# RMSNorm with ReLU: loads and stores on one hardware DMA queue in fixed order, 16-row chunks in place in f32, gamma spread on chip

## The chip, the cores and the metric

The kernel runs on one core of a Trainium2 chip. The metric is the device time of one execution in microseconds (us), lower is better. The span of the profile is shorter than the time by about 1.9 us (164.0 and 165.9 us for the kernel before), so large differences can be read from either.

## The reference

```python
x: (16, 1024, 512) f32;  gamma: (512,) f32, ones;  eps = 1e-5
rms = np.sqrt(np.mean(x ** 2, axis=-1, keepdims=True) + eps)
return np.maximum(x / rms * gamma, 0).astype(np.float32)
```

There are 16384 rows of 2 KB. 33.55 MB must be read and 33.55 MB written, 67.1 MB in all, for very little arithmetic.

## The kernel before

Each of the 128 partitions owns 128 neighbouring rows (256 KB). A chunk is 8 rows of every partition, 2 MB; there are 16 chunks. Loads are issued by SyncE (a hardware queue), stores by GpSimd (a software queue that also casts the bf16 result to f32). Gamma is broadcast to all partitions by one DMA at the head of the load queue.

```python
K = 8
gamma_bcast = bass.AP(tensor=gamma.tensor, offset=gamma.offset, ap=[[0, P], gamma.ap[0]])
nc.sync.dma_start(out=gamma_sbuf, in_=gamma_bcast)          # 128 reads of one 2 KB row
# ... cut: eps, scratch, gammaK (gamma repeated K times by a stride of 0)
for i in range(nchunks):                                    # pools of 4 buffers
    s = i * K
    nc.sync.dma_start(out=x_tile, in_=xv[:, s:s + K, :])
    nc.vector.tensor_mul(out=xg, in0=x_tile, in1=gammaK)
    for j in range(K):
        nc.scalar.activation(out=sq_scratch, in_=x_tile[:, j, :], func=Square, accum_out=ss[:, j:j+1])
    nc.scalar.activation(out=rms, in_=ss, func=Sqrt, bias=eps_sbuf, scale=inv_d)
    nc.vector.reciprocal(out=rstd, in_=rms)
    for j in range(K):
        nc.vector.tensor_scalar(out=o_tile[:, j, :], in0=xg[:, j, :], scalar1=rstd[:, j:j+1],
                                scalar2=0.0, op0=mult, op1=max)          # o_tile is bf16
    nc.gpsimd.dma_start(out=ov[:, s:s + K, :], in_=o_tile)               # casts to f32
```

## Time and profile before

| | before |
|---|---|
| time, median of 3 runs | 165.87 us (165.78 to 166.01) |
| span of the profile | 164.0 us |
| bytes moved, mean rate | 67.40 MB, 411 GB/s |
| DVE busy, ACT busy | 122.8 us, 99.4 us |

These lines are from the page of the kernel before. DVE is VectorE, ACT is ScalarE, POOL is GpSimd. The row of digits is the busy share of the 16 DMA engines in 40 equal slices of 4.1 us (9 is 90% or more), and the row under it is what they moved in each.

```profile
span 164.0 us, 565 instructions
DVE 122.8 (75%) x161; ACT 99.4 (61%) x274; POOL 8.9 (5%) x20
...
DMA  5999999999999999999999999999999999998994
GB/s 87 401 420 444 440 412 432 434 432 412 436 436 412 440 434 424 424 432 436 412 436 436 414 432 436 412 440 432 428 424 432 432 416 436 440 432 348 416 420 192
DMA packets 4755, 67.40 MB, mean 411 GB/s; under 512 B 528, under 2 KB 528, under 8 KB 656
...
q1 hardware_dynamic: 2448, 33.82, 57.4%
q0 software_dynamic: 2304, 33.56, 49.4%
...
HBM read 33.82 MB, written 33.55 MB: 411 GB/s over the span
```

The DMA engines are busy in every slice; no compute engine is near full. The first slice is slow (87 GB/s), and the slice at 148 to 152 us has a dip (348). Between them the rate is flat.

From the page's groups of instructions: out<-in, count, busy time, mean ns of one, idle before.

```profile
L70 DVE TENSOR_TENSOR xg<-x_tile,gamma_sbuf 128x4096 f32<-128x4096 f32 x16 | 70.5, 4406 | 29.3 <-DMA x_tile<-in_x_dram 29.3
L84 DVE TENSOR_SCALAR o_tile<-xg,rstd 128x512 bf16<-128x512 f32 x128 | 52.1, 480 | 0.1
```

### The profile page before, as it was taken

What the parts mean: (1) busy time and instruction counts of PE and PEld (TensorE: products, weight loads), DVE (VectorE), ACT (ScalarE), POOL (GpSimd) and SP (SyncE); (2) the same over time, 40 slices, a digit from 0 to 9 for tenths busy, and PEclk for the clock granted to TensorE, in tenths of its full rate; (3) what the DMA queues carried; (4) which work ended last, traced back from release to release, by engine and by line L of the source; (5) the groups of instructions that cost most, each with busy time, mean ns of one, the idle gap of its engine ahead of it and who ended that gap; (6) DMA issues with size and microseconds to landing.
All of it is one profiled execution on the core that took longest, in us unless ns stands there. A gap on an engine that the chain in (4) does not pass through costs nothing.

```text
span 164.0 us, 565 instructions
## 1 busy us (share of the span) xinstructions
DVE 122.8 (75%) x161; ACT 99.4 (61%) x274; POOL 8.9 (5%) x20
## 2 busy tenths in 40 slices
DVE  0029979999999999969498694968949498099600
ACT  3039999999993937739195682928649194094000
POOL 0000010011010101010100001010010101001100
DMA  5999999999999999999999999999999999998994
GB/s 87 401 420 444 440 412 432 434 432 412 436 436 412 440 434 424 424 432 436 412 436 436 414 432 436 412 440 432 428 424 432 432 416 436 440 432 348 416 420 192
DMA packets 4755, 67.40 MB, mean 411 GB/s; under 512 B 528, under 2 KB 528, under 8 KB 656
## 3 DMA queue, kind: packets, MB, share of 16 engines
q1 hardware_dynamic: 2448, 33.82, 57.4%
q0 software_dynamic: 2304, 33.56, 49.4%
q14 instruction: 3, 0.02, 0.0%
HBM read 33.82 MB, written 33.55 MB: 411 GB/s over the span
## 4 chain that ended last, share of the span: by engine, by line
issue 49%; DVE 27%; ACT 8%; DMA 6%; POOL 3%; POOLq 0%; SPq 0%
DVE xg L70 15%; DVE o_tile L84 11%; ACT sq_scratch L74 7%; DMA x_tile<-in_x_dram 6%; POOL out_dram L90 3%; ACT L77 1%; DVE rstd L80 1%; ACT rms L77 0%; POOLq L121 0%; SPq L48 0%; POOLq L90 0%
## 5 line engine op out<-in xcount | busy, mean ns | idle before, releaser
L74 ACT ACTIVATE sq_scratch<-x_tile 128x512 f32<-128x512 f32 x128 | 80.6, 630 | 48.8 <-DMA x_tile<-in_x_dram 45.3
L70 DVE TENSOR_TENSOR xg<-x_tile,gamma_sbuf 128x4096 f32<-128x4096 f32 x16 | 70.5, 4406 | 29.3 <-DMA x_tile<-in_x_dram 29.3
L84 DVE TENSOR_SCALAR o_tile<-xg,rstd 128x512 bf16<-128x512 f32 x128 | 52.1, 480 | 0.1
L74 ACT ACTIVATION_READ_ACCUMULATOR sq_scratch<-x_tile 128x1 f32 x128 | 23.9, 187 | 0.0
L90 POOL DMA_DIRECT2D out_dram<-o_tile x16 | 8.7, 541 | 145.9 <-DVE rstd L80 119.4
L77 ACT ACTIVATE rms<-ss,eps_sbuf 128x8 f32<-128x8 f32 x16 | 4.8, 301 | 0.5
L80 DVE RECIPROCAL rstd<-rms 128x8 f32<-128x8 f32 x16 | 3.1, 196 | 1.2 <-ACT rms L77 1.2
L74 ACT ACT_TABLE_LOAD x1 | 1.3, 1283 | 0.7 <-PEq L107 0.7
L77 ACT ACT_TABLE_LOAD x1 | 1.3, 1283 | 0.0
L51 DVE MEMSET eps_sbuf<- 128x1 f32 x1 | 0.1, 59 | 0.8 <-PEq L107 0.8
L107 POOL MEMSET const-float32-0.0<- 128x1 f32 x1 | 0.1, 99 | 0.2 <-issue 0.2
L107 POOL MEMSET const-bfloat16-1.0<- 128x1 bf16 x1 | 0.1, 102 | 0.0
L107 POOL MEMSET const-float32-1.0<- 128x1 f32 x1 | 0.1, 99 | 0.0
L107 POOL MEMSET const-uint8-127<- 128x1 uint8 x1 | 0.1, 99 | 0.0
## 6 DMA issues: line engine op xcount, KB each, us to landing
x_tile<-in_x_dram SPq DMA_DIRECT2D x16, 2048.0 KB, 26.4
out_dram<-o_tile POOLq DMA_DIRECT2D x16, 2048.0 KB, 21.3
gamma_sbuf<-in_gamma_dram SPq DMA_DIRECT2D x1, 256.0 KB, 5.4
```

Source lines behind the costliest of these rows:

```text
L51: nc.vector.memset(eps_sbuf, eps)
L70: nc.vector.tensor_mul(out=xg, in0=x_tile, in1=gammaK)
L74: nc.scalar.activation(out=sq_scratch, in_=x_tile[:, j, :], func=mybir.ActivationFunctionType.Square, accum_out=ssj)
L77: nc.scalar.activation(out=rms, in_=ss, func=mybir.ActivationFunctionType.Sqrt, bias=eps_sbuf, scale=inv_d)
L80: nc.vector.reciprocal(out=rstd, in_=rms)
L84: nc.vector.tensor_scalar(out=o_tile[:, j, :], in0=xg[:, j, :], scalar1=rj, scalar2=0.0, op0=mybir.AluOpType.mult, op1=mybir.AluOpType.max,)
L90: nc.gpsimd.dma_start(out=ov[:, s:s + K, :], in_=o_tile)
L107: nc = _bacc.Bacc("TRN2", target_bir_lowering=False, num_devices=1)
```

## The change

The intent is to keep the DMA engines in one direction at a time and never without work. All loads and stores go through SyncE's queue, in an order fixed by hand: six loads of 4 MB fill six slots, then store 0, store 1, load 6, store 2, load 7, stores 3 to 7. Chunks have 16 rows, and the work is done in place in f32, so no cast is needed. Gamma comes as four rows, one to partition 0, 32, 64 and 96, and a shuffle on DVE spreads each over its 32 partitions.

```diff
-    K = 8
+    K = 16
+    G = 8
+    nslots = 6
-    nc.sync.dma_start(out=gamma_sbuf, in_=gamma_bcast)
+    for q in range(0, P, 32):
+        nc.scalar.dma_start(out=gseed[q:q + 1, :], in_=gamma[None, :])
+    nc.vector.stream_shuffle(gamma_sb, gseed, [0] * 32)
# ... cut: tiles; the squares' scratch output is now in PSUM ("junk")
+    def load(i):
+        nc.sync.dma_start(out=slot[i % nslots], in_=xv[:, i * K:(i + 1) * K, :])
+    def store(i):
+        nc.sync.dma_start(out=ov[:, i * K:(i + 1) * K, :], in_=slot[i % nslots])
-        nc.gpsimd.dma_start(out=ov[:, s:s + K, :], in_=o_tile)
+    def compute(i):                     # in place in xt = slot[i % nslots], 8 rows at a time:
+        # 8 squares, Sqrt (ACT); xt *= gamma, reciprocal, 8 scalings with max 0 (DVE)
+    for i in range(min(nslots, nchunks)):
+        load(i)
+    for i in range(min(nslots, nchunks)):
+        compute(i)
+    nxt = nslots
+    for i in range(nchunks):
+        store(i)
+        if i >= 1 and nxt < nchunks:
+            load(nxt)
+            compute(nxt)
+            nxt += 1
```

More of the change, by code (lines that the diff above doesn't have):

```diff
@@ L6 @@
 from concourse._compat import with_exitstack
+F32 = mybir.dt.float32
+ALU = mybir.AluOpType
+ACTF = mybir.ActivationFunctionType
 @with_exitstack
@@ L23 @@
     n, d = x2.shape
-    assert n % P == 0
-    rows_per_part = n // P
+    rows = n // P
     inv_d = 1.0 / d
@@ L29 @@
     ov = out2.rearrange("(p r) d -> p r d", p=P)
-    K = 8
-    nchunks = rows_per_part // K
-    assert rows_per_part % K == 0
-    BF = mybir.dt.bfloat16
-    F32 = mybir.dt.float32
-    singles = ctx.enter_context(tc.tile_pool(name="singles", bufs=1))
-    pool = ctx.enter_context(tc.tile_pool(name="pool", bufs=4))
-    small = ctx.enter_context(tc.tile_pool(name="small", bufs=4))
-    gamma_sbuf = singles.tile([P, d], F32)
-    gamma_bcast = bass.AP(
-        tensor=gamma.tensor,
-        offset=gamma.offset,
-        ap=[[0, P], gamma.ap[0]],
-    )
@@ L48 @@
-    nc.sync.dma_start(out=gamma_sbuf, in_=gamma_bcast)
-    eps_sbuf = singles.tile([P, 1], F32)
-    nc.vector.memset(eps_sbuf, eps)
-    sq_scratch = singles.tile([P, d], F32)
-    gammaK = bass.AP(tensor=gamma_sbuf.tensor, offset=gamma_sbuf[:].offset,
-                     ap=[gamma_sbuf[:].ap[0], [0, K], gamma_sbuf[:].ap[1]])
-    for i in range(nchunks):
-        s = i * K
-        x_tile = pool.tile([P, K, d], F32)
-        nc.sync.dma_start(out=x_tile, in_=xv[:, s:s + K, :])
-        rstd = small.tile([P, K], F32)
-        rms = small.tile([P, K], F32)
-        ss = small.tile([P, K], F32)
-        xg = pool.tile([P, K, d], F32)
-        o_tile = pool.tile([P, K, d], BF)
-        nc.vector.tensor_mul(out=xg, in0=x_tile, in1=gammaK)
-        for j in range(K):
-            ssj = ss[:, j:j + 1]
-            nc.scalar.activation(out=sq_scratch, in_=x_tile[:, j, :],
-                                 func=mybir.ActivationFunctionType.Square,
-                                 accum_out=ssj)
-        nc.scalar.activation(out=rms, in_=ss,
-                             func=mybir.ActivationFunctionType.Sqrt,
-                             bias=eps_sbuf, scale=inv_d)
-        nc.vector.reciprocal(out=rstd, in_=rms)
-        for j in range(K):
-            rj = rstd[:, j:j + 1]
-            nc.vector.tensor_scalar(
-                out=o_tile[:, j, :], in0=xg[:, j, :],
-                scalar1=rj, scalar2=0.0,
-                op0=mybir.AluOpType.mult, op1=mybir.AluOpType.max,
-            )
-        nc.gpsimd.dma_start(out=ov[:, s:s + K, :], in_=o_tile)
@@ new lines @@
+    K = 16
+    G = 8
+    nchunks = rows // K
+    nslots = 6
+    ngroups = K // G
+    singles = ctx.enter_context(tc.tile_pool(name="singles", bufs=1))
+    slots = ctx.enter_context(tc.tile_pool(name="slots", bufs=1))
+    small = ctx.enter_context(tc.tile_pool(name="small", bufs=1))
+    psum = ctx.enter_context(
+        tc.tile_pool(name="psum", bufs=1, space=bass.MemoryType.PSUM))
+    ctx.enter_context(tc.manual_schedule())
+    gseed = singles.tile([P, d], F32, name="gseed")
+    gamma_sb = singles.tile([P, d], F32, name="gamma_sb")
@@ new lines @@
+    eps_sb = singles.tile([P, 1], F32, name="eps_sb")
+    junk = psum.tile([P, d], F32, name="junk")
+    slot = [slots.tile([P, K, d], F32, name=f"slot{s}") for s in range(nslots)]
+    ss = [small.tile([P, K], F32, name=f"ss{i}") for i in range(nchunks)]
+    rms = [small.tile([P, K], F32, name=f"rms{i}") for i in range(nchunks)]
+    rstd = [small.tile([P, K], F32, name=f"rstd{i}") for i in range(nchunks)]
+    def load(i):
+        nc.sync.dma_start(out=slot[i % nslots], in_=xv[:, i * K:(i + 1) * K, :])
@@ new lines, in store, with gammaG @@
+    def store(i):
+        nc.sync.dma_start(out=ov[:, i * K:(i + 1) * K, :], in_=slot[i % nslots])
+    def gammaG():
+        g = gamma_sb[:]
+        return bass.AP(tensor=g.tensor, offset=g.offset,
+                       ap=[g.ap[0], [0, G], g.ap[1]])
+    def compute(i):
+        xt = slot[i % nslots]
+        for g in range(ngroups):
+            a, b = g * G, (g + 1) * G
+            for j in range(a, b):
+                nc.scalar.activation(out=junk, in_=xt[:, j, :], func=ACTF.Square,
+                                     accum_out=ss[i][:, j:j + 1])
+            nc.scalar.activation(out=rms[i][:, a:b], in_=ss[i][:, a:b],
+                                 func=ACTF.Sqrt, bias=eps_sb, scale=inv_d)
+            nc.vector.tensor_mul(out=xt[:, a:b, :], in0=xt[:, a:b, :], in1=gammaG())
+            nc.vector.reciprocal(out=rstd[i][:, a:b], in_=rms[i][:, a:b])
+            for j in range(a, b):
+                nc.vector.tensor_scalar(
+                    out=xt[:, j, :], in0=xt[:, j, :],
+                    scalar1=rstd[i][:, j:j + 1], scalar2=0.0,
+                    op0=ALU.mult, op1=ALU.max)
@@ new lines @@
+    nc.vector.memset(gseed, 0.0)
+    nc.vector.memset(eps_sb, eps)
+    for q in range(0, P, 32):
[6 more added lines that the diff above has]
+    nxt = nslots
+    for i in range(nchunks):
+        store(i)
[3 more added lines that the diff above has]
+            nxt += 1
```

## The prediction

> What bounds the kernel: data movement. The page's slice row shows DMA at 9 or more nearly throughout and 411 GB/s over a span of 164.0 us; DVE is busy 122.8 us (75%), ACT 99.4 us (61%). 67.1 MB must move in any case. By the view of stretches, loads alone (11 to 24 us) ran at 432 GB/s, loads and stores mixed from two queues (70 to 110 us) at 427. At 432 the bytes take 155.4 us, so only 8.6 us are to be had:
> - start, about 3.7 us: the first packet starts at 1.75 us, full rate comes at 5.5, because gamma's 128 copies of a 2 KB row go first on the load queue. By the packet records 2.4 us worth of bytes is lost there;
> - mixing, about 1.3 us (1% of some 115 us);
> - a hole at 151 us, about 1.5 us: the last load's data ended at 139.1 us but its waiter on DVE started only at 143.1, DVE then needed 11.3 us, and the store queue ran dry;
> - end, 1.8 us from the last byte (162.15 us).
>
> What the change does. Gamma comes as four rows on ACT's queue and a shuffle on DVE: x loads start the load queue, 2 us won. One queue in fixed order doesn't mix directions: 1 us won. The last transfers are stores whose data is ready, so the hole goes: 1.5 us won. Stores read f32 instead of casting bf16; the HBM bytes are the same and I cost them the same. The Trainium skill ("DMA: Bandwidth & Descriptors", "Issuing engines are not separate DMA queues") says all queues run on the same 16 engines, so one queue can hold the full rate; the trace agrees (432 by one, 427 by two).
>
> Is compute early enough? In place, the multiplication by gamma must now wait for the eight squares of its half chunk. Per 8 rows DVE costs 4.43 + 0.12 + 3.25 us, period 7.57 us (chain of waits, 25 to 62 us); ACT 6.3 us. I expect scaling to f32 to cost what bf16 does (406 ns apart now): the skill ("VectorE: DVE Perf Modes", tier table) gives f32 tensor_scalar in SBUF a 2x mode. The first 4 MB land near 12.5 us, DVE starts near 18.8 us and finishes chunk i at 18.8 + 15.1(i+1): 34 us for the first, 140 us for the eighth. Transfers take 9.7 us each: six loads to 60, stores 0 and 1, load 6 (80 to 89), store 2, load 7 (99 to 109), stores 3 to 7, the last from 148 us. Every store's data is ready, the last by 8 us; load 6's wait for store 0 hides under store 1. DVE's work stays off the critical path.
>
> Sum: 1.75 + 0.5 ramp + 155.6 + 1.8 = 159.7 us of span; times are 1.9 us above the span now: 161.6, less 0.3 for the first issue coming 0.4 us earlier: 161.3 us, 2.8% less. Range 160.0 to 162.9.
>
> Shown right by: full rate by 3 us; slices near 432 GB/s to the end without a hole, 420 or more over the span; the eighth chunk's last scaling before 147 us; DVE busy about 122 us.
>
> Wrong if: scaling in place to f32 is slower (at 590 ns DVE would end near 165 us, the kernel above 175); f32 stores run below 431 GB/s; a turn between loads and stores (four) costs a bubble of 0.5 us or more; load 6 or 7 issues late. The margin over 2% is only 1.3 us, so a bubble or two makes it "same".
>
> Chances: faster 0.82, same 0.15, slower 0.03.

## More of the kernel before

The runs quoted are all at a granted clock of 1.0; the median of several runs is given, with the range or a 95% interval where it matters.

From the view of stretches of time of the kernel before: the stretch, its length, DVE's busy time, clock, DMA share, GB/s. Packets count where they start, so a short stretch is a few per cent off.

```profile
0.00:6.00 6.00, 0.06 (x1) 1.00 0.71 180
50.00:56.00 6.00, 6.00 (x11) 1.00 1.08 434
56.00:62.00 6.00, 6.00 (x8) 1.00 1.14 427
62.00:80.00 18.00, 16.24 (x24) 1.00 1.09 426
```

The first 6 us moved 180 GB/s: that is the start, with gamma's 128 small packets. The next three rows are the steady state with loads and stores interleaved; the stretch 56 to 62 us matters later.

## The result

| | before | after |
|---|---|---|
| time, median of 4 runs each | 165.82 us (165.5 to 166.01) | 164.6 us (164.31 to 164.98) |
| span of the profiled run | 164.0 us | 163.0 us |
| mean rate over the span | 411 GB/s | 412 GB/s |
| DVE busy, ACT busy | 122.8, 99.4 us | 124.6, 98.5 us |

The ratio is 0.9928 (95% interval 0.9907 to 0.9948): 0.7% faster, where 2.8% was predicted, and outside the predicted range. A ratio here is the mean time of one kernel's fast runs over the mean of the other's of the same rounds, so it is not quite the ratio of the medians. The profiled run was the slowest of the four; the others had spans of 162.2 to 162.9 us.

The page of the changed kernel:

```profile
span 163.0 us, 554 instructions
DVE 124.6 (76%) x164; ACT 98.5 (60%) x274; POOL 0.2 (0%) x4
...
DMA  7999899999999999999999999999999999999990
GB/s 249 394 459 443 386 466 434 404 458 426 434 458 396 450 322 394 442 434 418 460 410 426 402 434 434 450 402 434 434 434 426 426 442 434 434 442 426 434 394 24
DMA packets 2315, 67.14 MB, mean 412 GB/s; under 512 B 260, under 2 KB 260, under 8 KB 264
...
q1 hardware_dynamic: 2304, 67.11, 96.8%
```

The first slice is faster, as intended. There is a new dip near 57 to 65 us (322, 394), and almost nothing is moved in the last slice (24). The row of digits does not show the dip: an engine is "busy" during a slow packet too (the stretch of 333 GB/s shown below has a DMA share of 0.98). In a kernel bound by DMA, the row to watch is GB/s.

The compute lines, to set beside those of before:

```profile
L78 DVE TENSOR_TENSOR slot<-slot,gamma_sb 128x4096 f32<-128x4096 f32 x16 | 70.7, 4418 | 4.1 <-ACT junk L74 4.1
L81 DVE TENSOR_SCALAR slot<-slot,rstd 128x512 f32<-128x512 f32 x128 | 52.1, 480 | 0.6
```

The timeline of DVE and SyncE's queue from 139 us on (start, length, instruction):

```profile
139.63 3.25 DVE L81 TENSOR_SCALAR slot<-slot,rstd 128x512 f32<-128x512 f32 x8
142.91 0.33 SPq L62 DMA_DIRECT2D out_dram<-slot  x1
```

Compute did what was predicted. Scaling in f32 costs what it did in bf16. The last scaling ended at 142.9 us (140 predicted), and the last store was issued at once, 6 us before its turn on the queue. So compute is not what is missing.

The stretches of the changed kernel, the same as shown for before:

```profile
0.00:6.00 6.00, 0.49 (x2) 1.00 0.72 273
50.00:56.00 6.00, 5.96 (x7) 1.00 1.01 433
56.00:62.00 6.00, 6.00 (x6) 1.00 0.98 333
62.00:80.00 18.00, 17.89 (x28) 1.00 1.00 432
```

The same view, at the end of the changed kernel:

```profile
156.00:158.00 2.00, 0.00 (x0) 1.00 1.06 459
158.00:160.00 2.00, 0.00 (x0) 1.00 0.35 147
160.00:162.00 2.00, 0.00 (x0) 1.00 0.04 16
```

The start moved 273 GB/s in place of 180. From 56 to 62 us, while every buffer was full and every store's data was ready, the rate fell to 333. After 158 us few engines still worked, though there was no wait on anything.

The packet records of the trace show both places more finely. What follows from them was worked out from starts and lengths of packets, and from the times at which each DMA's 16 parts landed. A packet is 32 KB, and the usual one takes 1.213 us on its engine; the **loss** of a stretch is the sum of what its packets took beyond that, over 16 engines.

- Each engine handles 48 load packets before its first store packet. Packets 47 and 48, the last two loads, took 1.98 and 1.70 us on average, on all 16 engines. The loss is 1.26 us. The store packets after them are normal.
- The same happens, more weakly, to the last load packet before store 2 (0.41 us) and before store 3 (0.12 us). There is none where a load follows a store.
- The engines drift apart: the fifth load landed on its 16 engines within 0.9 us, the last store within 3.1 us. The distance had come to 3.1 us with load 7 and was not made up after it, so the kernel ends with the slowest engine.

The span, taken apart:

| term | predicted | measured (profiled run) |
|---|---|---|
| until the first packet | 1.75 | 1.75 |
| slow start | 0.5 | 0.55 |
| 67.1 MB at the steady rate | 155.6 | 154.9 (128 packets an engine at 1.210 us, 433 GB/s) |
| loss before stores (mean of the engines) | 0 | 1.8 (1.26 + 0.41 + 0.12) |
| slowest engine behind the mean at the end | 0 | 2.2 (last end 161.63, mean 159.45) |
| from the last byte to the end | 1.8 | 1.4 |
| sum | 159.7 | 162.6 of 163.0 |

The 0.4 us left are small packets and the engines' differing starts. So two terms are missing from the prediction, together 4 us. The experiments ask what makes them. (The expectations quoted below speak of slow "first packets" of the store and of a stall "at" the first store; that the slow packets are the last loads ahead of it was seen only afterwards.)

### The profile page after: what moved, and what is told of

It reads as the page before. It is cut to its first block, busy times and chain, and to the rows that moved or that the text cites. A ratio compares the mean times of both kernels' runs of the same rounds, so it can differ in the third digit from the quotient of the medians.

```text
span 163.0 us, 554 instructions
## 1 busy us (share of the span) xinstructions
DVE 124.6 (76%) x164; ACT 98.5 (60%) x274; POOL 0.2 (0%) x4
## 4 chain that ended last, share of the span: by engine, by line
DVE 74%; DMA 7%; ACT 3%; issue 2%; DVEq 0%
DVE slot L78 43%; DVE slot L81 30%; DMA slot<-in_x_dram 7%; ACT junk L74 3%; DVE rstd L79 1%; DVEq L133 0%
## 5 line engine op out<-in xcount | busy, mean ns | idle before, releaser
L74 ACT ACTIVATE junk<-slot 128x512 f32<-128x512 f32 x128 | 76.8, 600 | 24.4 <-DMA slot<-in_x_dram 20.9
L78 DVE TENSOR_TENSOR slot<-slot,gamma_sb 128x4096 f32<-128x4096 f32 x16 | 70.7, 4418 | 4.1 <-ACT junk L74 4.1
L81 DVE TENSOR_SCALAR slot<-slot,rstd 128x512 f32<-128x512 f32 x128 | 52.1, 480 | 0.6
L74 ACT ACTIVATION_READ_ACCUMULATOR junk<-slot 128x1 f32 x128 | 23.9, 186 | 0.0
L76 ACT ACTIVATE rms<-ss,eps_sb 128x8 f32<-128x8 f32 x16 | 4.8, 300 | 0.5
L86 DVE MEMSET gseed<- 128x512 f32 x1 | 0.5, 485 | 0.9 <-PEq L119 0.9
L93 DVE STREAM_SHUFFLE gamma_sb<-gseed 128x512 f32<-128x512 f32 x1 | 0.7, 723 | 0.0
```

Of the source, the lines that this page charges most:

```text
L74: nc.scalar.activation(out=junk, in_=xt[:, j, :], func=ACTF.Square, accum_out=ss[i][:, j:j + 1])
L76: nc.scalar.activation(out=rms[i][:, a:b], in_=ss[i][:, a:b], func=ACTF.Sqrt, bias=eps_sb, scale=inv_d)
L78: nc.vector.tensor_mul(out=xt[:, a:b, :], in0=xt[:, a:b, :], in1=gammaG())
L81: nc.vector.tensor_scalar(out=xt[:, j, :], in0=xt[:, j, :], scalar1=rstd[i][:, j:j + 1], scalar2=0.0, op0=ALU.mult, op1=ALU.max)
L86: nc.vector.memset(gseed, 0.0)
L93: nc.vector.stream_shuffle(gamma_sb, gseed, [0] * 32)
```

## The experiments

Ratios are against the kernel before in the same rounds. Four kernels ran together on one chip in each of the first four groups, and the last run alone.

### First group: is it the single queue, the number of turns, or compute?

**Stores back on the GpSimd queue**, all else as changed:

```diff
-        nc.sync.dma_start(out=ov[:, i * K:(i + 1) * K, :], in_=slot[i % nslots])
+        nc.gpsimd.dma_start(out=ov[:, i * K:(i + 1) * K, :], in_=slot[i % nslots])
```

> The changed kernel with only its stores put back on the GpSimd queue (f32, in place, gamma on chip, six slots kept). Theory (turning from loads to stores within one queue leaves each engine waiting, which a second queue fills): no packets of 1.5 us or more where the first store begins (32 KB packets on the single queue took 1.21 us in steady state and up to 2.4 us at the turn), the slices stay near 428 GB/s to the end, the slowest engine of the last store lands within about 1 us of the first, and the time is 161.5 to 163.5 us. Rival (in-place compute or f32 stores make the stores late or slow): still about 164.6 us or more, with the stall at the first store still there.

Measured: 163.05 us, ratio 0.9845 (0.9827 to 0.9863). The time and the rate are as the theory said, and the last store's landings are 1.8 us apart in place of 3.1 (about 1 was expected). But the theory fell in one point: there still is a loss, 0.97 us, at 36 to 40 us. It again falls on load packets, those just ahead of the first store's packets. Only the later ones are gone. So a second queue does not fill the first stall. The mixed stretch from 70 to 110 us ran at 433 GB/s here (view of stretches), so two queues as such do not cost the 1% that the prediction charged to mixing.

**Two turns in place of three** (a turn is a place where the queue goes from loads to stores):

```diff
-    for i in range(nchunks):
-        store(i)
-        if i >= 1 and nxt < nchunks: ...
+    store(0); store(1); load(6); load(7); compute(6); compute(7)
+    for i in range(2, nchunks):
+        store(i)
```

> Order changed to stores 0 and 1, loads 6 and 7, stores 2 to 7: two turns from loads to stores in place of three. Theory: the stall at the first store stays (about 1.26 us mean over the engines), the one at the second turn stays (about 0.4), the third goes (0.1), and the spread of the last store's 16 landings shrinks from 3.1 us to about 2.5; time 163.5 to 164.3 us. Rival (the stall belongs to the first write alone and the drift of the engines to something else): 164.6 us, spread 3.1 us.

Measured: 164.07 us, ratio 0.9904 (0.9883 to 0.9924). The losses are 1.36 and 0.24 us, the third is gone, and the last landings are 2.1 us apart. This is what the theory expects, but the interval overlaps that of the changed kernel (0.9907 to 0.9948), so the time alone does not show it.

**Five turns**, with 2 MB chunks:

```diff
-    K = 16
+    K = 8
-    nslots = 6
+    nslots = 12
```

> 8-row chunks in 12 slots on the one queue, same rule of order: five turns from loads to stores in place of three, transfers of 2 MB. Theory: each further turn costs 0.1 to 0.4 us mean and lets the engines drift further apart: 165 to 166.5 us, though compute starts about 5 us earlier (off the critical path). Rival (only the first write stalls): 164.6 us or a little less.

Measured: 165.88 us, ratio 1.0004 (0.9990 to 1.0019), slower than the changed kernel by 1.3 us. The time is in the theory's range, but not for its reason: the losses at 56 to 76 us sum to 1.4 us, and there is next to none at the turns after that. The last landings are 3.6 us apart. About 0.8 us of the difference is the smaller packet: in the steady stretch an engine needed 0.608 us for each 16 KB, which is 431 GB/s in place of 433. So a turn has no fixed price.

**No compute** (the result is wrong: x is stored as loaded):

```diff
-        compute(i)      # both places
```

> The changed kernel without its squares, multiplications and scalings: x is stored as loaded (result wrong on purpose), same DMA order. Theory: the same DMA timeline, the first-turn stall of about 1.3 us mean and the 3 us spread of the last landings included; 164 to 165 us. Rival (DVE and ACT traffic in SBUF or late stores cause the stalls): the stalls vanish and the time is 161 to 162 us.

Measured: 163.59 us, ratio 0.9871 (0.9858 to 0.9883), a little under both the 164 to 165 us of the theory and the time of the changed kernel. Two lines from its stretches, DVE idle:

```profile
50.00:56.00 6.00, 0.00 (x0) 1.00 1.00 431
56.00:62.00 6.00, 0.00 (x0) 1.00 0.98 328
```

The dip stands with no compute at all (328 GB/s; losses 1.30, 0.62 and 0.17 us). Compute, in-place writes and late stores are ruled out as its cause. The last landings are 2.0 us apart, not 3, so about 1 us of the final lag does go with compute; how, these runs do not show.

### Second group: first touch, addresses, or engines in step?

In the first group the later stalls were smaller where the engines had drifted apart. The rivals are a price of the first write to the output, and addresses. (Engines are called in step here when they end the same transfer within about 1 us of each other.)

**A store of zeros ahead of the loads**, 2 KB a partition, on the same queue:

```diff
+    nc.sync.dma_start(out=ov[:, 0:1, :], in_=zrow)     # zrow: [P, 1, d], zeroed
     for i in range(min(nslots, nchunks)):
         load(i)
```

> The changed kernel with a 256 KB store of zeros into the first row of every partition's share of the output, put ahead of the six loads on the same queue (it is overwritten by store 0). Theory of the first touch (the first write to a region of the output is what costs 1.26 us a engine at 57 to 62 us): the excess there falls under 0.4 us. Theory of the turn (each engine, all at the same moment, goes from reads to writes and its first packets run slow): the excess there stays at 1.1 to 1.4 us. Time: 0.6 us for the bytes plus about 1 us of turn-up at the start on top of 164.6 us by the second theory, about 164.5 by the first.

Measured: 166.35 us, ratio 1.0032 (1.0008 to 1.0056). The loss ahead of store 0 fell to 0.32 us, which spoke for the first touch; but its early packets were themselves quick (0.085 us each), and the start lost 0.7 us more. By the fifth load its engines were also 1.5 us apart, in place of 0.9, which matters below. The third group tries the same touch from another queue.

**Other addresses in HBM**, a chunk as one block of 4 MB:

```diff
-    xv = x2.rearrange("(p r) d -> p r d", p=P)
+    xv = x2.rearrange("(c p j) d -> c p j d", p=P, j=K)     # ov likewise
```

> Only the addresses in HBM change: a chunk is one contiguous 4 MB block (32 KB a partition, partitions adjacent) in place of 32 KB pieces 128 KB apart. If the slow first packets come of 16 engines that begin together at addresses a large power of two apart, the excess at the start (0.55 us) and at the first turn (1.26 us) changes by more than a third either way; if the turn itself costs the time, both stay within 20% and the time within 0.5% of 164.6 us.

Measured: 164.32 us, ratio 0.9909 (0.9894 to 0.9924). The start lost 0.70 us (up 27%), the first turn 0.97 (down 23%): neither "more than a third" nor "within 20%", so this is inconclusive. The engines were 1.4 us apart at the fifth load, so the smaller loss can come of that as well. Addresses are not the main cause of the first stall: most of it stays.

**Half of the engines put behind**:

```diff
+    for z in (4, 5):
+        nc.sync.dma_start(out=slot[z][0:8], in_=xv[0:8, z * K:(z + 1) * K, :])
     for i in range(min(nslots, nchunks)):
         load(i)
```

The Trainium skill ("DMA: Bandwidth & Descriptors", "Why a DMA increments its semaphore by 16 and not by 1") has a rule by which a DMA over 8 partitions runs on 8 of the 16 engines, and the packet records agree: 8 packets of 32 KB started within 0.6 us, and no other until one of them had ended.

> Two extra 256 KB loads over 8 partitions at the head of the queue, meant to put half of the engines 2.4 us behind the other half. If the stall at the first turn comes of all engines turning at once, its excess falls from 1.26 us to under 0.8 us (as the later, more staggered turns cost 0.4 and 0.1); if each engine pays for its own turn it stays at 1.2 to 1.35 us. The time is about 1 to 2 us longer in both cases, as the late half ends later.

Measured: 170.92 us, ratio 1.0308 (1.0293 to 1.0324). The start was much slower than meant (early 32 KB packets took 2 to 5 us), and that is the added time. But all three losses ahead of stores went: 0.07, 0.03 and 0.00 us. Two lines from its stretches:

```profile
50.00:56.00 6.00, 5.96 (x7) 1.00 1.01 437
56.00:62.00 6.00, 6.00 (x9) 1.00 1.01 433
```

A correction to what later expectations say: "9.6 us" was a mistake in grouping the landings. The fifth load landed within 3.1 us here.

**Two queues with 8-row chunks**, the edit of the first experiment and of the third together:

> Stores on the GpSimd queue as in two_queues, but 8-row chunks in 12 slots: packets of 16 KB as before. The kernel before had no stall at its first store, two_queues had 0.97 us with 32 KB packets. If the packet size makes the stall, it falls under 0.4 us here; if not (if the cast or another thing of the kernel before spared it), it stays near 1 us. Time 162.5 to 163.5 us, the rate about 431 GB/s in place of 433.

Measured: 164.03 us, ratio 0.9891 (0.9875 to 0.9908), slower than expected. The loss ahead of the first store is 1.19 us, so the packet's size does not make it. The stretch from 70 to 110 us ran at 430 GB/s with f32 stores; the kernel before, with its casting stores, moved 427 there.

### Third group: gamma and the first touch by themselves

**Only gamma changed**, in the kernel before:

```diff
-    nc.sync.dma_start(out=gamma_sbuf, in_=gamma_bcast)
+    gseed = singles.tile([P, d], F32)
+    nc.vector.memset(gseed, 0.0)
+    for q in range(0, P, 32):
+        nc.scalar.dma_start(out=gseed[q:q + 1, :], in_=gamma[None, :])
+    nc.vector.stream_shuffle(gamma_sbuf, gseed, [0] * 32)
```

> The kernel before with only gamma changed (four rows and a shuffle in place of the 128-row broadcast). Its engines will then be in step (landings of one load within 0.6 us; they were 1.9 us apart in the kernel before). If engines in step are what makes the first store stall, a stall of 0.7 us or more shows where the first store begins (the kernel before had 0.03 us there), and of the 1.6 us won at the start less than 1 us is left: 164.7 to 165.9 us. If the kernel before was spared by its bf16 stores, no stall: 164.0 to 164.5 us.

Measured: 163.86 us, ratio 0.9883 (0.9871 to 0.9896). This part alone gains more than the whole change. Its loads landed within 0.8 us in place of 1.9, and a loss appeared where the first store begins (0.38 us, in place of 0.04), smaller than the 0.7 expected; the time is better than either theory said. The hole near 151 us went as well: its last load was used from 136.2 us on instead of 143.1. The stretches around its first store:

```profile
20.00:25.00 5.00, 5.00 (x10) 1.00 1.02 436
25.00:29.00 4.00, 4.00 (x6) 1.00 1.01 383
```

The same stretches of the kernel before:

```profile
20.00:25.00 5.00, 3.80 (x11) 1.00 0.98 419
25.00:29.00 4.00, 4.00 (x2) 1.00 1.08 438
```

**Gamma's broadcast put back** in the changed kernel:

```diff
-    for q in range(0, P, 32):
-        nc.scalar.dma_start(out=gseed[q:q + 1, :], in_=gamma[None, :])
-    nc.vector.stream_shuffle(gamma_sb, gseed, [0] * 32)
+    nc.sync.dma_start(out=gamma_sb, in_=gamma_bcast)      # ahead of the loads
```

> The changed kernel with the broadcast of gamma put back at the head of the load queue. The engines will be about 1.9 us apart. If being in step makes the stall, the excess at the first turn falls from 1.26 us to under 0.8 us, and the time is within 1 us of 164.6 us although the start loses 1.6 us. If not, the stall stays and the time is 165.8 to 166.5 us.

Measured: 165.77 us, ratio 1.0003 (0.9990 to 1.0016). Its stretches:

```profile
0.00:6.00 6.00, 0.49 (x2) 1.00 0.61 191
50.00:56.00 6.00, 6.00 (x9) 1.00 1.00 427
56.00:62.00 6.00, 5.96 (x11) 1.00 1.01 437
```

The loss at the first turn went from 1.26 to 0.03 us: where the changed kernel moved 333 GB/s, this one moved 437. The time is 1.2 us worse, just outside the theory's "within 1 us" and at the edge of the rival's range: the start costs more again, the second turn still lost 0.45 us, and the last landings are still 3.2 us apart.

**The early touch from GpSimd's queue**, beside the first load, in the changed kernel and in the one with two queues:

```diff
+    zrow = singles.tile([P, 1, d // 4], F32, name="zrow")
+    nc.vector.memset(zrow, 0.0)
+    nc.gpsimd.dma_start(out=ov[:, 0:1, 0:d // 4], in_=zrow)
```

> The changed kernel plus one store of 512 bytes a partition to the first row of every partition's share of the output, from the GpSimd queue during the first load (overwritten later). The engines stay in step. If the first touch of the output's region costs the time, the excess at the first turn falls under 0.5 us and the time is 163.2 to 164.2 us; if engines in step cost it, it stays at 1.1 to 1.4 us and the time at 164.6.

> The same early touch, in the kernel with stores on the GpSimd queue (163.05 us, stall 0.97 us at its first store). First touch: the stall falls under 0.4 us and the time is 162.0 to 162.7 us. Engines in step: unchanged, 163.0 us.

Measured: 165.27 us, ratio 0.9971 (0.9956 to 0.9987), and 163.46 us, ratio 0.9869 (0.9850 to 0.9888). The first time is 0.7 us above what either theory said, and the cause of that was not sought; the losses stand at 1.46 and 0.84 us. So the first touch of the output is not the cause. The smaller loss with the store on the same queue (0.32 us) came with engines that were further apart (1.5 us, against 1.0 in the first run here).

### Fourth group and last run: distance by itself, and the second queue

**A small and a middling lag** for half of the engines, 4 and 10 rows:

```diff
+    nc.sync.dma_start(out=slot[5][0:8, 0:4, :], in_=xv[0:8, 5 * K:5 * K + 4, :])    # small
+    nc.sync.dma_start(out=slot[5][0:8, 0:10, :], in_=xv[0:8, 5 * K:5 * K + 10, :])  # middling
```

> The changed kernel with one extra load of 4 rows over 8 partitions at the head of the queue, to put half of the engines about 1 us behind (the earlier stagger of two 16-row loads put them 9.6 us apart). Theory (the slow last load packets before a turn come of engines that turn in step; less in step, less stall): the excess at the first turn lies between those of the changed kernel (1.26 us, landings 0.9 us apart) and of the one with the broadcast put back (0.03 us, 1.8 us apart): 0.1 to 0.9 us. Rival (the broadcast and the large stagger removed the stall in another way than by the engines' distance): 1.1 us or more. Time 164.5 to 166 us.

Measured: 165.40 us, ratio 0.9979 (0.9965 to 0.9993). It missed its aim: the fifth load landed within 1.0 us (the next expectation says 0.7), so the loss of 1.26 us is what engines in step have. It still serves as a control: an extra DMA at the head does not take the stall away.

> As small_stagger with 10 rows in place of 4: small_stagger missed its aim, its engines came back into step during the slow start (landings 0.7 us apart before the turn) and its stall stayed at 1.26 us. Here the aim is landings 1.5 to 5 us apart before the first turn. If that is reached: by the theory the excess on the last load packets before the first store is under 0.5 us; by the rival 1.0 us or more. If the landings are under 1.2 us apart the run says nothing. Time 166 to 169 us.

Measured: 165.57 us, ratio 0.9989 (0.9972 to 1.0006), under the range expected. Here the aim was met, 1.7 us apart, and the loss at the first turn is 0.03 us. Its stretches:

```profile
50.00:56.00 6.00, 6.00 (x8) 1.00 1.01 433
56.00:62.00 6.00, 5.96 (x11) 1.00 1.01 437
```

The first stall is gone and yet the time is no better. The start lost about 1.4 us in place of 0.55, the second and the third turn still lost 0.27 and 0.22 us, and there the distance grew from 1.8 us (store 1) to 2.7 (load 6) and 3.3 (load 7); it was 3.2 for the last store. The stretch with the second turn, in the changed kernel, in gamma_back and in mid_stagger:

```profile
85.00:95.00 10.00, 9.93 (x17) 1.00 1.00 416
85.00:95.00 10.00, 9.96 (x11) 1.00 1.00 413
85.00:95.00 10.00, 9.96 (x11) 1.00 0.99 416
```

So putting the engines apart took away the first stall, but not the second.

**Gamma in one DMA on four engines**, with two queues:

```diff
-    for q in range(0, P, 32):
-        nc.scalar.dma_start(out=gseed[q:q + 1, :], in_=gamma[None, :])
+    nc.scalar.dma_start(out=<rows 0, 32, 64, 96 of gseed>, in_=<gamma, four times>)
```

> Two queues with gamma's four rows in one DMA on four engines in place of four DMAs on one engine. If gamma's small packets are part of why one engine lands 1.5 us after the mean in two_queues, the lag of the slowest shrinks by 0.3 us and the time is 162.6 to 162.9 us; if not, 163.05 us.

Measured: 163.15 us, ratio 0.9852 (0.9833 to 0.9872), the last landings 1.9 us apart: no effect. Gamma's small packets are not the lag.

**Stores on the Activation queue**:

```diff
-        nc.sync.dma_start(out=ov[:, i * K:(i + 1) * K, :], in_=slot[i % nslots])
+        nc.scalar.dma_start(out=ov[:, i * K:(i + 1) * K, :], in_=slot[i % nslots])
-    # compute(0) to compute(5), then the loop shown in the change
+    compute(0); compute(1); compute(2)
+    for i in range(nchunks):
+        store(i)
+        if i + 3 < nchunks:
+            if i + 3 >= nslots:
+                load(i + 3)
+            compute(i + 3)
```

> Stores on the Activation queue instead of GpSimd, each issued after the squares of the third chunk further on. Theory (two queues are needed, whoever feeds the second): as two_queues, 162.5 to 163.5 us, with a stall of up to 1 us where the first store starts among loads. If the GpSimd queue was what saved two_queues its turns, 164 us or more.

Measured: 162.84 us (162.47 to 163.14), ratio 0.9824 (0.9810 to 0.9837). This is the best version; it beats both kernels. From its page, the rate by slice and the two hardware queues:

```profile
GB/s 260 391 440 464 399 439 464 401 423 472 407 407 458 309 423 439 439 423 439 439 417 447 431 415 456 431 407 464 431 399 472 431 399 472 431 390 472 439 390 138
...
q1 hardware_dynamic: 1152, 33.55, 49.3%
q10 hardware_dynamic: 1160, 33.56, 48.3%
```

Its last stretches:

```profile
156.00:158.00 2.00, 0.00 (x0) 1.00 1.10 475
158.00:160.00 2.00, 0.00 (x0) 1.00 0.04 16
```

It has the stall once, where its first store begins (309; loss 1.13 us), and none later. Its engines end together: the last landings are 1.4 us apart, and after 158 us there is nearly nothing left (16 GB/s, where the changed kernel moved 147). So a second queue brings the gain, and it need not be GpSimd's. (With two queues loads and stores also mix, which these runs do not separate from the queue itself.)

**The changed kernel again**, on the chip of this group:

> The changed kernel itself, on the same chip as the others: 164.6 us, excess at the first turn 1.0 to 1.5 us, the last landings 2 to 3.1 us apart.

Measured: 164.84 us, ratio 0.9943 (0.9927 to 0.9959); losses 1.17, 0.29 and 0.13 us; the last landings 3.1 us apart. It repeats.

### The single-queue runs side by side

"Apart" is the time between the first and the last engine's landing of that transfer. The fifth load is the last transfer that lands before the first turn, and store 1 the last before the second (in fewer_turns load 6 still comes between).

| run | fifth load apart, us | loss at the first turn, us | store 1 apart, us | loss at the second turn, us | last store apart, us |
|---|---|---|---|---|---|
| no_compute | 0.51 | 1.30 | 0.58 | 0.62 | 1.97 |
| after, after_again | 0.91, 0.90 | 1.26, 1.17 | 1.42, 1.58 | 0.41, 0.29 | 3.07, 3.13 |
| touch_one | 1.02 | 1.46 | 1.17 | 0.58 | 2.71 |
| small_stagger | 1.02 | 1.26 | 1.24 | 0.34 | 3.35 |
| fewer_turns | 1.07 | 1.36 | 1.24 | 0.24 | 2.15 |
| contiguous | 1.44 | 0.97 | 2.10 | 0.06 | 2.84 |
| early_store | 1.50 | 0.32 | 0.84 | 0.51 | 2.58 |
| mid_stagger | 1.74 | 0.03 | 1.80 | 0.27 | 3.24 |
| gamma_back | 1.77 | 0.03 | 1.73 | 0.45 | 3.20 |
| stagger | 3.10 | 0.07 | 3.29 | 0.03 | 3.25 |

At the first turn the loss is about one packet (1.2 us) where the engines are up to 1.1 us apart, smaller at 1.4 to 1.5 us, and gone from 1.7 us on. The two sides were reached in different ways, with and without the broadcast. The second turn has no such limit at 1.7 us: its loss is 0.62 us at most, falls with the distance only roughly, and is nearly gone (0.06 and 0.03 us) only in the two runs that were more than 2 us apart.

## Why the prediction was wrong

- **The failing step** was "Every store's data is ready", taken to mean that the queue then runs at the full rate: the sum has no term for the turn from loads to stores, and none for the slowest engine. The prediction named a bubble at a turn of 0.5 us or more as what would make it wrong, and gave it too little weight. (It counted four turns; its order has three from loads to stores and two back.) The runs showed 1.26, 0.41 and 0.12 us at the three turns to stores, none at the turns back, and 2.2 us of waiting for the slowest engine.
- **"2 us won" at the start: right in kind, and then largely lost.** Gamma alone gained 2.0 us (163.86 us). In the changed kernel the bytes lost at the start fell as expected, but without the broadcast the engines run in step, and engines in step stall at the first turn (1.26 us; 0.03 with the broadcast back). The slow broadcast had hidden this in the kernel before, where the loads landed 1.9 us apart and the loss at the first store was 0.04 us.
- **"One queue in fixed order doesn't mix directions: 1 us won": wrong as to the cause.** Mixed f32 traffic on two queues ran at 433 GB/s, the same as one direction alone. The 427 of before goes with its 16 KB packets and casting stores: with f32 stores of 16 KB the stretch had 430, and with only gamma changed it had 427 still. The gain in rate was there (154.9 us for the bytes in place of 155.6), but not through the order. The stretch in the kernel before, in gamma_only, in two_q_k8 and in two_queues (DVE, ACT and POOL busy, clock, DMA share, GB/s):

```profile
70.00:110.00 40.00, 31.35 (x43) 24.36 (x68) 2.67 (x5) 1.00 1.10 427
70.00:110.00 40.00, 32.49 (x41) 24.83 (x71) 2.13 (x4) 1.00 1.08 427
70.00:110.00 40.00, 34.73 (x45) 24.84 (x71) 2.13 (x4) 1.00 1.00 430
70.00:110.00 40.00, 39.82 (x54) 24.48 (x70) 1.07 (x2) 1.00 1.00 433
```

- **"The hole goes": right**, but gamma alone took it away too.
- **Compute off the critical path: right.** DVE ended at 142.9 us (140 predicted, at a period of 7.74 us in place of 7.57), and the scaling in f32 took 3.25 us for eight, as in bf16. The prediction rested this on the Trainium skill's tier table ("VectorE: DVE Perf Modes"), which gives f32 tensor_scalar in SBUF a 2x mode; the run agrees in so far as the scaling is no slower than before.
- **Fixed order on one queue: a loss.** With the stores of the same kernel on a second queue (ACT's, with its work reordered to issue them) it takes 162.84 us against 164.84 in the same group; with only the queue changed (GpSimd's, in another group) it took 163.05 us. One stall is left in place of three, and the engines end 1.4 us apart in place of 3.1. The prediction cited the skill ("Issuing engines are not separate DMA queues") that all queues run on the same 16 engines. The steady rate agrees (433 GB/s either way), but it does not follow that one queue loses nothing.

Shown: the stall needs no compute; it does not depend on an earlier touch of the output; at the first turn it is there whole with engines up to 1.1 us apart and gone with 1.7 us or more. Open: why the engines, in step, take longer for the last loads ahead of a store; why later turns differ from the first and from run to run; and which engines lag, for the records do not name them. That the stalls drive the engines apart is read from the landings but was not isolated. In the changed kernel the distance was 0.9 us before the first turn, 1.2 after it (load 5), 2.6 after the second (load 6) and 3.1 after the third (load 7). In gamma_back, with the first stall gone, it was 1.7 to 1.8 us up to store 1 and 3.2 from load 6 on, where the second turn lost 0.45 us. In stagger, with no loss at any turn, it stayed between 3.0 and 3.3 us from the fifth load to the end.

## What to carry to other kernels

When DMA is the limit, add two terms to bytes over rate: what the queue loses where it turns from loads to stores, and how far the slowest engine is behind the mean at the end, and look for both in GB/s by slice and in the spread of the last landings, since the busy share shows neither. A second queue for the stores was worth 1.2% here over a hand-ordered single one, though both have the same engines and the same steady rate. Undo each part of a change by itself: here the smallest part, gamma, was worth more alone than the whole.

## What the Trainium skill lacked or had wrong

- "DMA: Bandwidth & Descriptors", rules for kernel authors, says that spreading DMAs over issuing engines for bandwidth "Doesn't help". The steady rate agrees (433 GB/s with one queue or two), but loads and stores on two hardware queues took 162.84 us and on one 164.84 us.
- No page that was read here has the stall ahead of stores: with engines 0.9 us apart, the last two 32 KB load packets before the first store took 1.98 and 1.70 us in place of 1.21.
- No page that was read here says how far the engines drift apart or that the distance decides the stall: the last store's 16 parts landed 2.0 to 3.6 us apart on one queue, and the loss at the first turn was 1.26 us with engines 0.9 us apart and 0.03 with 1.7.
- "DMA: Bandwidth & Descriptors" gives no cost for a small row broadcast to all partitions at the head of a queue: 128 reads of 2 KB took 5.4 us from issue to landing, and without them the kernel before is 2.0 us faster.
- "ScalarE: Activation LUTs" has a note that ScalarE writes PSUM faster than SBUF, and the note has no figure: the 128x512 square took 600 ns to PSUM and 630 to SBUF.
